# A decoder block's column stage: three engines' order written by hand, two threshold searches advanced by a budget

## The chip, the cores and the metric

One Trainium2 chip, one of its cores. A core has TensorE (matrix products; PE in the profile, PEld its weight loads), VectorE (DVE), ScalarE (ACT), GpSimd (POOL) and SyncE (SP), which issues most transfers. The metric is the device time of one execution in microseconds (us). Before: 1518.09 us, the median of 3 runs (1517.33 to 1519.06).

## The reference, cut to what matters

A decoder block over 1024 tokens of 1024 features: a sparse attention branch (an indexer scores all earlier tokens, and each query attends only to its 256 best) and a gated short convolution are merged by sigmoid gates; then 32 experts of a two-level router.

```
proj = h @ w_in
q, k, v, qi, ki, wi, conv_in, conv_b, conv_c, gates = split(proj)
rel = relu(einsum('bqhd,bsd->bqhs', qib, ki) * 64 ** -0.5)
score = einsum('bqhs,bqh->bqs', rel, wib) * 8 ** -0.5        # where admissible
_, idx = lax.top_k(score, 256)                               # attention over idx only
conv = conv_b * short_conv(conv_c * conv_in, conv_w)         # width 3, per channel
g_attn, g_conv = split(sigmoid(gates + gate_bias))
merged = g_attn * (attn @ w_attn_up) + g_conv * (conv @ w_conv_up)
h = layer_norm(alpha * h + merged @ w_out)
h = layer_norm(alpha * h + experts(h))                       # 32 experts, top 2 of a group
```

## The kernel before, in words

Matrix products run in three parts for precision: each operand is split into a high part (a rounding copy on ScalarE) and a low part (raw minus high, on VectorE or GpSimd). `mm3` (lines 141 to 144) issues high by high, high by low (of the tokens) and low by high. Eight pairs `xh`, `xl` hold the transposed input in the pool `big`, whose 16 pages (tag `er`) later hold raw expert weights.

The order of the stages: projections of keys, values and indexer; scores `sc` for query blocks 2 to 7 (per head and 512 keys two matmuls, a Relu `rl` on ScalarE, line 277, and an accumulation into `score` on VectorE, line 281); the **column stage**; attention, with eight more columns (`gattn`) as filling work for TensorE; merge, normalisation, router; experts, whose weights stream from memory.

The column stage computes 128 output columns of `w_in` at a time for all tokens. Column j is loaded by `load_col` (raw `cr`, high part `ch` on ScalarE at line 129, low part `cl` on GpSimd at line 133, both into pages of tag `w`, of which there are five) and multiplied by `proj_col`: two halves of 512 tokens, 24 matmuls each, into a PSUM bank `pc`, which `use` then reads out. The program runs over the columns 0, 1, then 3, 4, 2, then 6, 7, 5, then 9, 10, 8, then 11, and then 12 to 19. Of a convolution triple, the first (`conv_c`) is copied out by ScalarE into `cc`; the second (`conv_in`) is multiplied into `cc` by VectorE, which then forms the three-tap filter `y` (lines 435 to 437); the third (`conv_b`), one triple late, is multiplied into `y` by VectorE and split into `convh` (ScalarE) and `convl` (GpSimd). A gate column 12 to 19 is read out through a Sigmoid into `g` by ScalarE (line 460), and is followed by 24 matmuls `pu` of the convolution with an up-projection weight `uw` (copy on ScalarE, low part on GpSimd). With eight such tiles the stage has 20 x 48 + 8 x 24 = 1152 matmuls.

The indexer's 256 best of a query are found by a threshold: `topk` bisects 16 bits of the score's upper half, then 16 of the lower. It runs twice: for blocks 2, 3, 4 by counting on VectorE (`count`, line 346), for blocks 5, 6, 7 by sums of signs on ScalarE (`sign_sums`, line 320: three sums of 768, 896 and 1024 elements and six activations of one column for each bit), with preparation and a final pass (lines 395 to 401) on VectorE. Both are issued with a late priority (`prio(LATE)`) behind the column stage in the program; the framework's scheduler chooses the order of each engine in this stage from priorities and its own model, so that the searches fill what is free. From attention on, TensorE's order is the program's (`manual_schedule`).

PSUM tiles come in tags: `f` (2 banks), `l` (3), `tr` (2), `pv` (1). The scores and the columns both take `l`.

Of the kernel before, what the change touches and what calls it, by code (L numbers as in the profile page):

```python
# [11 lines left out]
I16 = mybir.dt.int16  # L12
# [33 lines left out]
ROWS_AT = (0, 4)  # L46
HOLD = 50
NSQ = 2
OHB = 8
# [23 lines left out]
def build(tc, I, out):  # L73
# [224 lines left out]
    def topk(blocks, scalar=False):  # L298
# [7 lines left out]
        if not scalar:  # L306
            acc = psf("acc", (P, ng), "pv")
        hi, lo, msk = [tmp(n, I32) for n in ("thi", "tlo", "msk")]
# [9 lines left out]
        def sign_sums(dt, b, o):  # L318
            for i in range(ng):
                nc.scalar.activation(signs[:, :L[i]], key[i].bitcast(dt), AF.Sign, bias=b[:, i:i + 1], scale=1.0,  # L320
                                     accum_out=o[:, i:i + 1])

        def descend_signs(name, base, dt, above=None):
# [8 lines left out]
            for bit in range(15, -1, -1):  # L332
                sign_sums(dt, b, total)
                for i in range(ng):
                    nc.scalar.activation(sign[:, i:i + 1], total[:, i:i + 1], AF.Sign, bias=least[:, i:i + 1],
                                         scale=1.0)
                if bit:
                    for i in range(ng):
                        nc.scalar.activation(b[:, i:i + 1], sign[:, i:i + 1], AF.Identity, bias=b[:, i:i + 1],
                                             scale=-float(1 << bit) / 2)  # L340
# [3 lines left out]
        def count(op, dt, c, o):  # L344
            for i in range(ng):
                V.tensor_scalar(junk[:, :L[i]], key[i].bitcast(dt), c[:, i:i + 1], None, op0=op, op1=OP.add,
                                accum_out=o[:, i:i + 1])

        def descend(name, base, dt, above=None):
            if scalar:  # L350
                return descend_signs(name, base, dt, above)
            c = tmp(name)
            V.memset(c, base + 32768.0)
            for bit in range(15, -1, -1):
                count(OP.is_ge, dt, c, cnt)
                if above is not None:
                    V.tensor_tensor(cnt, cnt, above, op=OP.add)
                step = float(1 << bit)
# [3 lines left out]

        for i, t in enumerate(blocks):
            h = score[t].bitcast(I16)[:, 1::2]
            m = scratch[:, :L[i]].bitcast(I16)
            V.tensor_scalar(m, h, 0.0, 32767.0, op0=OP.is_lt, op1=OP.mult)
            V.tensor_tensor(key[i].bitcast(I16), h, m, op=OP.bitwise_xor)
        th = descend("th", -32768.0, I16)
        above = tmp("above")
        if scalar:  # L370
            V.tensor_scalar(acc, th, -1.0, -0.5, op0=OP.mult, op1=OP.add)
            sign_sums(I16, acc, above)
        else:
            count(OP.is_gt, I16, th, above)
        V.tensor_scalar(neg, th, 0.0, None, op0=OP.is_lt)
        V.tensor_scalar(sg, neg, -2.0, 1.0, op0=OP.mult, op1=OP.add)
        V.tensor_scalar(off, neg, 65535.0, None, op0=OP.mult)
        for i, t in enumerate(blocks):
            low = score[t].bitcast(U16)[:, 0::2]
            V.tensor_scalar(scratch[:, :L[i]], low, sg[:, i:i + 1], off[:, i:i + 1], op0=OP.mult, op1=OP.add)  # L380
            V.scalar_tensor_tensor(key[i], key[i].bitcast(I16), th[:, i:i + 1], scratch[:, :L[i]], op0=OP.is_equal,
                                   op1=OP.mult)
        tl = descend("tl", 0.0, U16, above)
        V.tensor_copy(hi, th)
# [6 lines left out]
        for i, t in enumerate(blocks):  # L391
            s = score[t]
            T = hi.bitcast(F32)[:, i:i + 1]
            jk, cm = scratch[:, :L[i]], key[i]
            V.tensor_scalar(jk, s, T, None, op0=OP.is_gt, op1=OP.add, accum_out=cnt[:, i:i + 1])
            V.tensor_scalar(jk, s, T, None, op0=OP.is_equal)
            V.tensor_scalar(need[:, i:i + 1], cnt[:, i:i + 1], -1.0, float(TOPK), op0=OP.mult, op1=OP.add)
            V.tensor_tensor_scan(cm, jk, jk, 0.0, op0=OP.add, op1=OP.bypass)
            V.scalar_tensor_tensor(cm, cm, need[:, i:i + 1], jk, op0=OP.is_le, op1=OP.mult)
            V.scalar_tensor_tensor(s, s, T, cm, op0=OP.is_gt, op1=OP.add)  # L400
            nc.scalar.activation(s, s, AF.Copy, bias=NEG, scale=-NEG)


# [7 lines left out]
    def proj_col(j, use):  # L411
        h, l = load_col(j)
        for n in range(2):
            c = slice(n * 512, n * 512 + 512)
            p = psf("pc", tag="l")
            for k in range(KT):
                mm3(p, h[:, k], l[:, k], xh[k][:, c], xl[k][:, c], k == 0, k == KT - 1)
            use(p, c)

# [37 lines left out]
    def gconv_tile(j):  # L457
# [4 lines left out]
        for n in range(2):  # L462
            c = slice(n * 512, n * 512 + 512)
            p = psf("pu")
            for _ in up_half(uw, lambda k: convh[k][:, c], lambda k: convl[k][:, c], n, p):
                pass
            nc.vector.tensor_tensor(g[:, c], p, g[:, c], op=OP.mult)  # L467
        nc.sync.dma_start(gc_d[j], g)
# [43 lines left out]

    for c in range(5):
        if c < 4:
            conv_in(c)
        if c > 0:
            conv_out(c - 1)
    for j in range(8):
        gconv_tile(j)

# [83 lines left out]

    with prio(LATE):
        topk([5, 6, 7], True)
        topk([2, 3, 4])
    tensor_order = ExitStack()
# [773 lines left out]
```

## Time and profile before

| | |
|---|---|
| median of 3 runs | 1518.09 us |
| profiled execution, its own time | 1517.83 us |
| its span, first to last instruction | 1516.0 us |
| mean granted TensorE clock | 0.966 |
| PE busy | 1416.2 us (93%) |
| DVE busy | 1101.3 us (73%) |
| ACT busy | 997.2 us (66%) |
| POOL busy | 399.6 us (26%) |

Busy shares are means over stages with different limits, so they don't say what a change in one stage is worth; the rows further below are of the column stage and its neighbours. A bracket in a row of the timeline gives the idle time before the instruction and what ended it. A busy TensorE is not TensorE at full speed: its clock has two levels, and matmuls overlap, so that their pitch (start to start) and not their duration is what a column costs.

### The profile page before, as it was taken

The page shows a single profiled execution, that of the slowest core. Times are in us where ns is not written, and L with a number is a line of the kernel's source. Part 1 is how long each engine was busy: PE and PEld are TensorE (multiplying, and loading weights), DVE is VectorE, ACT ScalarE, POOL GpSimd, SP SyncE. Part 2 cuts the span into 40 slices and gives each one's busy share as a digit, 9 for nine tenths or more (in the row PEclk, how much of TensorE's full clock was granted, in tenths as well). Part 3 has the DMA queues.
Part 4 walks back from the last instruction along what each step waited for, and adds up shares of the span by engine and source line. Part 5 has one row for each costly group of instructions (what it writes and reads, how often), then busy time and mean ns, then how long its engine had stood idle before and what let it go on. Part 6 is the DMA issues. An engine that isn't in the chain of part 4 may idle for free. (4 is left out here: it accounts for less than half of the span.)

```text
span 1516.0 us, 20432 instructions
## 1 busy us (share of the span) xinstructions
PE 1416.2 (93%) x6746; PEld 1158.7 (76%) x6746; DVE 1101.3 (73%) x1913; ACT 997.2 (66%) x1657; POOL 399.6 (26%) x346
## 2 busy tenths in 40 slices
PE   7999899899998999988999499999999999999993
PEld 7887687678877888866788477777777777777773
DVE  5354999960616666657634889889998889888876
ACT  5444788589326666555432378888888888888864
POOL 2433112232324555324000511111111111111106
PEclk9999899999999999989999699999999999999997
DMA  5201211112112121335854678999999999999942
GB/s 192 70 21 58 88 44 42 42 42 84 56 65 75 50 84 57 105 119 180 303 205 171 238 260 273 362 365 369 365 372 364 367 360 362 360 357 363 365 196 112
DMA packets 97053, 301.78 MB, mean 199 GB/s; under 512 B 14670, under 2 KB 19150, under 8 KB 96944
## 3 DMA queue, kind: packets, MB, share of 16 engines
q1 hardware_dynamic: 88160, 284.28, 51.1%
q0 software_dynamic: 8784, 16.16, 4.3%
q8 instruction: 54, 0.88, 0.2%
q14 instruction: 55, 0.45, 0.1%
HBM read 276.12 MB, written 40.11 MB: 209 GB/s over the span
## 5 line engine op out<-in xcount | busy, mean ns | idle before, releaser
L133 DVE TENSOR_TENSOR el<-er,eh 128x1024 fp32r<-128x1024 f32 x376 | 447.6, 1222 | 52.6 <-ACT eh L129 47.5
L129 ACT ACTIVATE eh<-er 128x1024 fp32r<-128x1024 f32 x376 | 390.7, 1062 | 62.8 <-PE gu L144 31.1
L142 PE MATMUL gu<-eh,exh 128*128 128x512 f32 x512 | 208.4, 407 | 0.0
L144 PE MATMUL gu<-eh,exl 128*128 128x512 f32 x512 | 202.9, 396 | 0.0
L143 PE MATMUL gu<-el,exh 128*128 128x512 f32 x512 | 202.7, 396 | 0.0
L142 PE MATMUL pc<-xh,ch 128*128 128x512 f32 x448 | 180.7, 403 | 11.0 <-DVE cc L433 8.9
L144 PE MATMUL pc<-xh,cl 128*128 128x512 f32 x448 | 175.8, 395 | 1.3 <-POOL cl L133 1.3
L143 PE MATMUL pc<-xl,ch 128*128 128x512 f32 x448 | 176.8, 395 | 0.0
L1044 POOL DMA_INDIRECT y_d<-yo,gidx x29 | 46.1, 1588 | 436.8 <-ACT yo L1036 422.5
L144 PEld LDWEIGHTS gu<-eh,exl 128*128 128x128 f32 x512 | 96.4, 188 | 23.4 <-DVE exl L133 0.2
L143 PEld LDWEIGHTS gu<-el,exh 128*128 128x128 f32 x512 | 96.8, 189 | 20.4
L142 PEld LDWEIGHTS gu<-eh,exh 128*128 128x128 f32 x512 | 96.7, 189 | 20.6 <-ACT exh L129 0.4
L142 PEld LDWEIGHTS pc<-xh,ch 128*128 128x128 f32 x448 | 85.3, 190 | 26.9 <-DVE cc L433 9.8
L133 POOL TENSOR_TENSOR cl<-cr,ch 128x1024 fp32r<-128x1024 f32 x28 | 67.4, 2408 | 138.5 <-PE pc L144 119.0
L142 PE MATMUL py<-eh,hT 128*128 128x512 f32 x256 | 101.3, 396 | 0.0
L143 PE MATMUL py<-el,hT 128*128 128x512 f32 x256 | 101.2, 395 | 0.0
L144 PE MATMUL py<-eh,hT 128*128 128x512 f32 x256 | 101.2, 395 | 0.0
L144 PEld LDWEIGHTS pc<-xh,cl 128*128 128x128 f32 x448 | 85.3, 190 | 20.5 <-POOL cl L133 1.8
L559 POOL TENSOR_TENSOR p<-p,mx 128x128 f32<-128x128 f32 (+7 forms) x64 | 73.0, 1148 | 92.7 <-DVE mx L558 56.2
L143 PEld LDWEIGHTS pc<-xl,ch 128*128 128x128 f32 x448 | 85.4, 191 | 13.7
L281 DVE SCALAR_TENSOR_TENSOR score<-rl,wis,score 128x512 f32<-128x512 f32 (+1 forms) x70 | 51.0, 750 | 34.6 <-ACT rl L277 33.4
L467 DVE TENSOR_TENSOR g<-pu,g 128x512 f32<-128x512 f32 x16 | 11.0, 689 | 84.5 <-ACT g L460 43.5
(336 smaller groups left out, 3105.1 us busy)
## 6 DMA issues: line engine op xcount, KB each, us to landing
er<-in_w_e SPq DMA_DIRECT2D x384, 512.0 KB
cr<-in_w_ct SPq DMA_DIRECT2D x28, 512.0 KB
gc_d<-g SPq DMA_DIRECT2D x8, 512.0 KB
ga_d<-g SPq DMA_DIRECT2D x8, 512.0 KB
ur<-in_w_au SPq DMA_DIRECT2D x16, 256.0 KB
gg<-ga_d SPq DMA_DIRECT2D x16, 256.0 KB
gg<-gc_d SPq DMA_DIRECT2D x16, 256.0 KB
wor<-in_w_out SPq DMA_DIRECT2D x8, 512.0 KB
```

The costliest lines, as they stand in the source:

```text
L129: exps["last"] = nc.scalar.activation(hi, src, AF.Copy).ins
L133: i = eng.tensor_tensor(lo, src, hi.bitcast(F32), op=OP.subtract)
L142: nc.tensor.matmul(ps, sh, mh, start=start, stop=False)
L143: nc.tensor.matmul(ps, sh, ml, start=False, stop=False)
L144: return nc.tensor.matmul(ps, sl, mh, start=False, stop=stop).ins
L281: nc.vector.scalar_tensor_tensor(sc[:, n0:n1], rl, wis[:, t, h:h + 1], sc[:, n0:n1], op0=OP.mult, op1=OP.add)
L467: nc.vector.tensor_tensor(g[:, c], p, g[:, c], op=OP.mult)
L559: nc.gpsimd.tensor_tensor(p[:, :L], p[:, :L], mx[:, 0:1].to_broadcast([P, L]), op=OP.mult)
L1044: nc.gpsimd.indirect_dma_start(out=y_d, out_offset=bass.IndirectOffsetOnAxis(ap=si, axis=0), in_=yo, in_offset=None, bounds_check=S - 1, o ...
```

## The change

Three parts. The column stage goes into a block in which TensorE, VectorE and ScalarE all run in the program's order (GpSimd and the transfers stay with the scheduler). The two searches become generators: they yield, before each step, the engine and an estimated cost, and `search(2.8)`, called in the middle and at the end of each half projection of the columns from 2 on and after each half of `pu`, advances both until 2.8 us x 0.6 of ScalarE or 2.8 us x 0.8 of VectorE are spent; what is left runs after the last tile. And the columns 0, 1, 3 and 4 take PSUM tag `f`, and the raw pages of columns 0 and 1 take tag `w`, so that neither waits for what the scores use. A small part: the `above` counts of the VectorE search are kept in PSUM (`over`).

```diff
+SHARE = {"act": 0.6, "dve": 0.8}
+EARLY_COLS = (0, 1, 3, 4)
...
         def sign_sums(dt, b, o):
             for i in range(ng):
+                yield "act", 0.45 + L[i] / 1000
                 nc.scalar.activation(signs[:, :L[i]], key[i].bitcast(dt), AF.Sign, bias=b[:, i:i + 1], scale=1.0,
                                      accum_out=o[:, i:i + 1])
...
             for bit in range(15, -1, -1):
-                sign_sums(dt, b, total)
+                yield from sign_sums(dt, b, total)
...
         def count(op, dt, c, o):
             for i in range(ng):
+                yield "dve", 0.4 + L[i] / 1000
                 V.tensor_scalar(junk[:, :L[i]], key[i].bitcast(dt), c[:, i:i + 1], None, op0=op, op1=OP.add,
                                 accum_out=o[:, i:i + 1])
...
+    searches = {}
+
+    def search(us):
+
+        left = {n: us * SHARE[n] + searches.get(n, 0.0) for n in SHARE}
+        for name in ("scalar", "vector"):
+            while name in searches:
+                gen, step = searches[name]
+                if step is not None:
+                    if left[step[0]] <= 0:
+                        break
+                    left[step[0]] -= step[1]
+                step = next(gen, None)
+                searches[name] = gen, step
+                if step is None:
+                    searches.pop(name)
+        for n in SHARE:
+            searches[n] = min(0.0, left[n])
...
     def proj_col(j, use):
-        h, l = load_col(j)
+        h, l = load_col(j, "w" if j < 2 else "a")
         for n in range(2):
             c = slice(n * 512, n * 512 + 512)
-            p = psf("pc", tag="l")
+            p = psf("pc", tag="f" if j in EARLY_COLS else "l")
             for k in range(KT):
                 mm3(p, h[:, k], l[:, k], xh[k][:, c], xl[k][:, c], k == 0, k == KT - 1)
+                if k == KT // 2 - 1 and j > 1:
+                    search(2.8)
+            if j > 1:
+                search(2.8)
             use(p, c)
...
             for _ in up_half(uw, lambda k: convh[k][:, c], lambda k: convl[k][:, c], n, p):
                 pass
+            search(2.8)
             nc.vector.tensor_tensor(g[:, c], p, g[:, c], op=OP.mult)
...
-    for c in range(5):
-        if c < 4:
-            conv_in(c)
-        if c > 0:
-            conv_out(c - 1)
-    for j in range(8):
-        gconv_tile(j)
+    searches["vector"] = topk([2, 3, 4]), None
+    searches["scalar"] = topk([5, 6, 7], True), None
+    with tc.manual_schedule(engines={ET.PE, ET.DVE, ET.Activation}):
+        for c in range(5):
+            if c < 4:
+                conv_in(c)
+            if c > 0:
+                conv_out(c - 1)
+        for j in range(8):
+            gconv_tile(j)
+        search(1.0e6)
...
-    with prio(LATE):
-        topk([5, 6, 7], True)
-        topk([2, 3, 4])
```

On ScalarE, where columns 0 and 1 of the kernel before are under way (the two `cc` are column 0's halves), the order of before has the second read-out of column 0 and behind it a `ch`, which is that of column 4, the fourth in the program's order; the `ch` of columns 0, 1 and 3 stand further up.

```order
L320 ACTIVATE signs,ths_3208<-keys,thb_3207 128x768
L339 ACTIVATE thb_3207<-thg_3209,thb_3207 128x1
L320 ACTIVATE signs,ths_3208<-key,thb_3207 128x896
L335 ACTIVATE thg_3209<-ths_3208,thl_3210 128x1
L432 ACTIVATE cc<-pc 128x512
L129 ACTIVATE ch<-cr 128x1024
L320 ACTIVATE signs,ths_3208<-key,thb_3207 128x1024
```

After the change, on ScalarE at the end of column 6 (its two `cc`) and the start of column 7, the next in the program's order:

```order
L324 ACTIVATE signs,ths_1889<-key,thb_1888 128x1024
L339 ACTIVATE thg_1890<-ths_1889,thl_1891 128x1 x3
L343 ACTIVATE thb_1888<-thg_1890,thb_1888 128x1 x3
L324 ACTIVATE signs,ths_1889<-keys,thb_1888 128x768
L469 ACTIVATE cc<-pc 128x512
L131 ACTIVATE ch<-cr 128x1024
L324 ACTIVATE signs,ths_1889<-key,thb_1888 128x896
```

The `ch` behind the second `cc` is now that of the column that TensorE takes next. At every other boundary it is the same: the `ch` of a column stands behind all that the column before it put on ScalarE, for columns 3i + 2 behind `convh convh`, for a gate column behind the second `g`, the sums of two `search` calls and the `uw` copy.

On VectorE after the change, behind the end of column 4 (the two last of the filter's three operations) up to where column 2's first half is read out (`y<-pc`):

```order
L473 SCALAR_TENSOR_TENSOR y<-cc,cw,y 128x1023
L474 SCALAR_TENSOR_TENSOR y<-cc,cw,y 128x1022
L351 TENSOR_SCALAR junk,cnt_1863<-keys,th_1938 128x640
L366 TENSOR_SCALAR acc<-cnt_1863 128x3
L367 SCALAR_TENSOR_TENSOR th_1938<-acc,th_1938 128x3
L351 TENSOR_SCALAR junk,cnt_1863<-keys,th_1938 128x384
L351 TENSOR_SCALAR junk,cnt_1863<-keys,th_1938 128x512
L351 TENSOR_SCALAR junk,cnt_1863<-keys,th_1938 128x640
L366 TENSOR_SCALAR acc<-cnt_1863 128x3
L367 SCALAR_TENSOR_TENSOR th_1938<-acc,th_1938 128x3
L351 TENSOR_SCALAR junk,cnt_1863<-keys,th_1938 128x384
L483 TENSOR_TENSOR y<-pc,y 128x512
```

Ahead of the filter stands the last `cc<-pc` of column 4; behind this `y<-pc` follow two counts with two small operations, a whole bit (three counts, two small operations) and the `y<-pc` of column 2's second half. In the order of before, the counts had no fixed place beside the columns.

On TensorE before, column 0 begins behind the last of 64 score matmuls of blocks 6 and 7:

```order
L274 MATMUL sc<-kiT,qiT 128x512
L275 MATMUL sc<-kiT,qiT 128x512
L142 MATMUL pc<-xh,ch 128x512
L143 MATMUL pc<-xl,ch 128x512
L144 MATMUL pc<-xh,cl 128x512
```

After the change, column 0 begins ahead of those 64, right behind the projections `pj`:

```order
L146 MATMUL pj<-wh,xl 128x512
L144 MATMUL pc<-xh,ch 128x512
L145 MATMUL pc<-xl,ch 128x512
L146 MATMUL pc<-xh,cl 128x512
L144 MATMUL pc<-xh,ch 128x512
L145 MATMUL pc<-xl,ch 128x512
L146 MATMUL pc<-xh,cl 128x512
L276 MATMUL sc<-kiT,qiT 128x512
L277 MATMUL sc<-kiT,qiT 128x512
L144 MATMUL pc<-xh,ch 128x512
L276 MATMUL sc<-kiT,qiT 128x384
L277 MATMUL sc<-kiT,qiT 128x384
```

The 144 matmuls of columns 0, 1 and 3 are now spread among the 64; the last eight score matmuls stand behind the last matmul of column 3, and column 4 behind them.

## Rows read from the trace of the kernel before

**Rows 1.** Busy time by stage: scores, first columns, the rest of the column stage.

```profile
144.70:173.30 28.60, 22.84 (x65) 13.85 (x63) 26.36 (x36) 19.56 (x34) 7.37 (x6) 0.76 0.31 101
173.30:206.10 32.80, 32.80 (x145) 27.14 (x145) 31.31 (x79) 28.52 (x73) 4.82 (x2) 1.00 0.20 65
206.10:335.00 128.90, 116.61 (x494) 94.30 (x493) 117.44 (x296) 93.32 (x236) 36.12 (x20) 0.96 0.13 42
335.00:452.20 117.20, 117.20 (x520) 96.89 (x519) 31.93 (x42) 63.43 (x146) 27.51 (x16) 1.00 0.19 68
```

The columns are the stretch and its length, then busy us and instructions of PE, PEld, DVE, ACT and POOL, the granted clock, the share of the transfer engines and GB/s.

**Rows 2.** Timeline of PE: start, us, instruction; the first column.

```profile
173.33 0.50 PE L142 MATMUL pc<-xh,ch 128*128 128x512 f32 x1
173.67 0.39 PE L143 MATMUL pc<-xl,ch 128*128 128x512 f32 x1
...
179.81 0.39 PE L143 MATMUL pc<-xl,ch 128*128 128x512 f32 x1
```

**Rows 3.** Timeline of ACT: two copies `ch`, one bit of the sign search.

```profile
148.00 1.06 ACT L129 ACTIVATE ch<-cr 128x1024 fp32r<-128x1024 f32 x1 [0.77 <-DMA cr<-in_w_ct]
...
185.00 0.59 ACT L432 ACTIVATE cc<-pc 128x512 f32<-128x512 f32 x1
185.48 1.06 ACT L129 ACTIVATE ch<-cr 128x1024 fp32r<-128x1024 f32 x1
...
188.29 0.93 ACT L320 ACTIVATE signs<-keys,thb 128x768 int16<-128x768 int16 x1
...
190.61 1.15 ACT L320 ACTIVATE signs<-key,thb 128x1024 int16<-128x1024 int16 x1
...
192.48 0.93 ACT L320 ACTIVATE signs<-keys,thb 128x768 int16<-128x768 int16 x1
```

**Rows 4.** Timeline of POOL: low parts of columns and of the convolution.

```profile
149.14 2.36 POOL L133 TENSOR_TENSOR cl<-cr,ch 128x1024 fp32r<-128x1024 f32 x1 [0.75 <-ACT ch L129]
...
195.40 2.42 POOL L133 TENSOR_TENSOR cl<-cr,ch 128x1024 fp32r<-128x1024 f32 x1 [8.47 <-PE pc L144]
...
231.18 1.29 POOL L133 TENSOR_TENSOR convl<-y,convh 128x512 fp32r<-128x512 f32 x1 [11.61 <-ACT convh L129]
232.44 2.40 POOL L133 TENSOR_TENSOR cl<-cr,ch 128x1024 fp32r<-128x1024 f32 x1
```

**Rows 5.** Groups by line and shape, 140 to 470 us: busy us, mean ns.

```profile
L129 ACT ACTIVATE convh<-y 128x512 fp32r<-128x512 f32 x8 | 5.0, 627 | 18.7 <-DVE y L446 18.7
...
L446 DVE TENSOR_TENSOR y<-pc,y 128x512 f32<-128x512 f32 x8 | 5.5, 681 | 0.0
...
L437 DVE SCALAR_TENSOR_TENSOR y<-cc,cw,y 128x1022 f32<-128x1022 f32 x4 | 5.1, 1281 | 0.0
...
L367 DVE TENSOR_TENSOR key<-score,signs 128x896 int16<-128x896 int16 x1 | 1.1, 1084 | 0.0
```

**Rows 6.** Timeline of DVE: score accumulations, then one bit of the counts.

```profile
149.47 3.68 DVE L281 SCALAR_TENSOR_TENSOR score<-rl,wis,score 128x384 f32<-128x384 f32 x3 [0.53 <-ACT rl L277]
...
156.26 0.75 DVE L281 SCALAR_TENSOR_TENSOR score<-rl,wis,score 128x512 f32<-128x512 f32 x1 [0.20 <-ACT rl L277]
...
181.33 0.61 DVE L346 TENSOR_SCALAR_CACHE_REDUCE junk<-keys,th 128x384 uint16<-128x384 int16 x1
...
184.09 0.61 DVE L346 TENSOR_SCALAR_CACHE_REDUCE junk<-keys,th 128x384 uint16<-128x384 int16 x1
```

**Rows 7.** Timeline of PE behind its longest wait in the column stage.

```profile
299.55 0.79 PE L142 MATMUL pc<-xh,ch 128*128 128x512 f32 x1 [6.09 <-DVE cc L433]
...
303.12 0.39 PE L144 MATMUL pc<-xh,cl 128*128 128x512 f32 x1
```

**Rows 8.** Timeline of ACT: a wait, and the copy behind it.

```profile
389.98 0.85 ACT L401 ACTIVATE score<-score 128x768 f32<-128x768 f32 x1 [5.80 <-DVE score L400]
390.73 1.04 ACT L129 ACTIVATE ch<-cr 128x1024 fp32r<-128x1024 f32 x1
```

**Rows 9.** Instructions on the expert weights' raw pages: issues, ns, first and last start.

```profile
L1077 SPq DMA_DIRECT2D er<-in_w_e x380: 327/328/1165, 735.0 to 1443.0; - x190
```

More of the change, by code (lines that the diff above doesn't have):

```diff
@@ L306, in topk @@
         if not scalar:
-            acc = psf("acc", (P, ng), "pv")
+            pa = psf("acc", (P, 2 * ng), "pv")
+            acc, over = pa[:, :ng], pa[:, ng:]
         hi, lo, msk = [tmp(n, I32) for n in ("thi", "tlo", "msk")]
@@ L350, in descend @@
             if scalar:
-                return descend_signs(name, base, dt, above)
+                return (yield from descend_signs(name, base, dt, above))
             c = tmp(name)
+            if above is not None:
+                V.tensor_copy(over, above)
             V.memset(c, base + 32768.0)
             for bit in range(15, -1, -1):
-                count(OP.is_ge, dt, c, cnt)
+                yield from count(OP.is_ge, dt, c, cnt)
                 if above is not None:
-                    V.tensor_tensor(cnt, cnt, above, op=OP.add)
+                    V.tensor_tensor(cnt, cnt, over, op=OP.add)
                 step = float(1 << bit)
@@ L363, in topk @@
         for i, t in enumerate(blocks):
+            yield "dve", L[i] / 500
             h = score[t].bitcast(I16)[:, 1::2]
@@ L367, in topk @@
             V.tensor_tensor(key[i].bitcast(I16), h, m, op=OP.bitwise_xor)
-        th = descend("th", -32768.0, I16)
+        th = yield from descend("th", -32768.0, I16)
         above = tmp("above")
@@ L371, in topk @@
             V.tensor_scalar(acc, th, -1.0, -0.5, op0=OP.mult, op1=OP.add)
-            sign_sums(I16, acc, above)
+            yield from sign_sums(I16, acc, above)
         else:
-            count(OP.is_gt, I16, th, above)
+            yield from count(OP.is_gt, I16, th, above)
         V.tensor_scalar(neg, th, 0.0, None, op0=OP.is_lt)
@@ L379, in topk @@
             low = score[t].bitcast(U16)[:, 0::2]
+            yield "dve", L[i] / 400
             V.tensor_scalar(scratch[:, :L[i]], low, sg[:, i:i + 1], off[:, i:i + 1], op0=OP.mult, op1=OP.add)
@@ L382, in topk @@
                                    op1=OP.mult)
-        tl = descend("tl", 0.0, U16, above)
+        tl = yield from descend("tl", 0.0, U16, above)
+        yield "dve", 1.5
         V.tensor_copy(hi, th)
@@ L394, in topk @@
             jk, cm = scratch[:, :L[i]], key[i]
+            yield "dve", L[i] / 300
             V.tensor_scalar(jk, s, T, None, op0=OP.is_gt, op1=OP.add, accum_out=cnt[:, i:i + 1])
             V.tensor_scalar(jk, s, T, None, op0=OP.is_equal)
+            yield "dve", L[i] / 300
             V.tensor_scalar(need[:, i:i + 1], cnt[:, i:i + 1], -1.0, float(TOPK), op0=OP.mult, op1=OP.add)
             V.tensor_tensor_scan(cm, jk, jk, 0.0, op0=OP.add, op1=OP.bypass)
+            yield "dve", L[i] / 300
             V.scalar_tensor_tensor(cm, cm, need[:, i:i + 1], jk, op0=OP.is_le, op1=OP.mult)
             V.scalar_tensor_tensor(s, s, T, cm, op0=OP.is_gt, op1=OP.add)
+            yield "act", L[i] / 800
             nc.scalar.activation(s, s, AF.Copy, bias=NEG, scale=-NEG)
+    searches = {}
[14 more added lines that the diff above has]
+            searches[n] = min(0.0, left[n])
     def load_col(j, rtag="a"):
```

## The prediction

> **What bounds the kernel now.** I read the busy times by stage first. In the column stage TensorE is the bound: in its second half it is busy 117.2 us of 117.2 at full clock, in its first 32.8 us it never stops, and only between 206.1 and 335.0 does it stand idle, 12.3 us of 128.9 [rows 1]. The timeline of PE gives its pitch at full speed: 27 matmuls start between 173.67 and 179.81, which is 0.2274 us each [rows 2]. The stage's 1152 matmuls are worth 262.0 us at that pitch; from 173.33 to 452.2 they took 278.9. So 16.9 us are lost, all behind the first three columns (144 x 0.2274 = 32.7 us, which ends at 206.1).
>
> In the stretch ahead of it, the scores of blocks 6 and 7, VectorE sets the pace: busy 26.4 us of 28.6, while TensorE works 22.8 us at a mean granted clock of 0.76 [rows 1]. Here TensorE's time is nearly free: 64 score matmuls take 28.6 us that need some 13.7.
>
> What the reader should see next is how far ahead of TensorE the columns are split. Column 4 starts on TensorE at 206.1; its `ch` is made at 185.48 [rows 3], its `cl` at 195.40 [rows 4]. The split leads its column by ten to twenty us. This lead is what the new order touches.
>
> **The change, part by part.** *The scores.* The 144 matmuls of columns 0, 1 and 3 move between the score matmuls. TensorE then has 32.7 + 13.7 = 46.5 us of work from 144.7 on and is the bound, so it ends at 191.2; between columns 0 and 1 the chain read-out, `ch`, `cl` (below, 4.3 us) is covered for 2.5 us by score matmuls, so 193.0. Before, this work was done at 206.1: 13.1 us are won. But column 4 cannot start then. ScalarE's order ahead of `ch` of column 4 begins with a sign sum, which needs VectorE's keys of blocks 5 to 7 and, behind them, the memsets. VectorE ends the scores about 1.5 us after TensorE (a Relu, an accumulation of 0.75 [rows 6]); then come one filter operation of 1.28 and the keys, three operations of 1.08 [rows 5], three that I take at 0.6 and small ones of 0.7 in all, 7.0 together: 201.6. Then ScalarE: four sign sums, six small activations, two read-outs `cc` and `ch`. One bit of three sums and six small activations takes 4.19 (188.29 to 192.48), of which the small ones are 1.1; a fourth sum is 0.9, the read-outs go at 0.5 (185.00 to 185.48) and `ch` is 1.06 [rows 3]: 7.2 us, 208.8. `cl` takes 2.4 and starts 0.08 behind its `ch` (148.00 + 1.06 to 149.14) [rows 3, 4]. Its third matmul starts at 211.3, and as two need no `cl`, column 4 starts in effect at 210.8: **4.7 us later** than the 206.1 of before. Bounds: 13 us earlier if the hole were filled, some 8 later if the scores run slower.
>
> *Boundaries behind a ScalarE read-out* (columns 3i to 3i + 1; three of them behind column 4). ScalarE waits for TensorE's last matmul, reads out (0.59), makes `ch` (1.06) [rows 3], GpSimd makes `cl` (2.40) [rows 4], three hand-overs of 0.08, less the two matmuls (0.45): 3.84 us in which TensorE stands. Three are **11.5**.
>
> *Boundaries behind a convolution output* (2 to 6, 5 to 9, 8 to 11). VectorE's `y` (0.68), `convh` (0.63) [rows 5], `convl` (1.26 from start to start), `cl` (2.40) [rows 4], hand-overs 0.33, less 0.45: 4.85. On top VectorE is late. From the end of column 4 it has to do `cc` (0.6), the filter (3.1, from 1.28 an operation [rows 5]), a count of 640 with its small ones (1.3), a bit (2.76, 181.33 to 184.09 [rows 6]), a count (0.65), `y` (0.6), then 2.1 for two counts and 2.76 for a bit: 13.9 us, where column 2 takes 48 x 0.2274 = 10.9. So its last `y` starts 3.0 late; for columns 5 and 8, where the budget cuts the bits elsewhere, 2.4 and 2.1. Three boundaries: **22.1**. Behind column 11 there is also the low part of `uw` (as `convl`, 1.3), and `y` stands behind counts that follow a wait for ScalarE's thirty-second sum, 3.1 late: **9.3**. The remaining boundaries (4 to 2, 7 to 5, 10 to 8) cost nothing: the column ahead is read out by VectorE, so `ch` waits only for 7 us of sums, which fit in the 10.9.
>
> *Gate tiles.* Behind a column ScalarE reads out `g` (0.6), does one bit (4.19), `uw` (0.55), GpSimd the low part (1.3) and `cl` (2.4), with hand-overs 9.3; TensorE has 24 matmuls `pu` (5.46) and two of the next column (0.45): it stands 3.4 behind tiles 12, 14, 16. Behind 13, 15, 17 the bit lacks its sum of 896 (1.0): 2.4. Behind 18 `uw` and `ch` stand behind `score5`, which waits until VectorE has read out the first half of `pu` and done two more operations (some 5.2 behind the column) and takes 0.85 [rows 8]: 5.2 + 0.85 + 0.55 + 1.3 + 2.4, less 5.46 and 0.45, is 4.4. **21.8.**
>
> *The clock.* Behind the 6.09 us wait TensorE made 8 matmuls in 3.57 us (299.55 to 303.12) [rows 7], half its full clock (1.2 for 2.4 GHz), where 1.82 is due: 1.75 a long wait. Eight long waits (column 4's, three, four): 14.0. For the seven at the tiles, two short waits each, I find no row; between 0 and 1.75 I take 0.6: 4.2. **18.2.**
>
> *Attention's start.* About a dozen VectorE operations of the final pass land among its first units. Between nothing (TensorE has filling columns) and 8 us I take **2**, nearer to nothing as the operations stand one by one between others. The PSUM copy of `above` and the loads of two columns ahead of time cost nothing: VectorE and the queues wait for the columns.
>
> **Sum**: 4.7 + 11.5 + 22.1 + 9.3 + 21.8 + 18.2 + 2.0 = 89.6; the loss of 16.9 falls away: **+72.7**. The profiled execution took 1517.8, the median is 1518.1: I predict **1590**.
>
> **Rivals.** *Smaller.* VectorE is not late (its counts run while TensorE stands), and no wait but the bare ones counts: 4.7 + 11.5 + 14.6 + 6.2 + 21.8 - 16.9 = +41.9, **1560**. For it: waits give VectorE time to catch up. Against: the filter is at the end of a column with no wait behind it.
>
> *Larger.* `cl` and VectorE get in each other's way. Three accumulations beside a `cl` took 3.68 us, 1.23 each, where one alone takes 0.75 [rows 4, 6]; 1.7 us on each of 14 boundaries is +24, **1614**. Against: only operations like those, which read two tiles, show it; the bit from 181.33 was beside none. [...]
>
> *Faster.* ScalarE does the copy `ch` ahead of the read-out, since its inputs have long landed. Then nothing but the columns' own work is left: 13.1 won at the scores and the 16.9 lost before, **1488**. It decides below (16.9 - 4.7) / 14 = 0.87 us a boundary; one `cl` alone is 2.40. Against: at 389.98 ScalarE stood 5.80 us for `score`, and `ch` came right behind it, not during the wait [rows 8]. The Trainium skill (TensorE: Matmul & The Clock Gate, the table at its head) calls ScalarE's queue a strict FIFO. By that rule this rival is out; the trace agrees, with the 5.80.
>
> *No change.* The delay is taken up later, since the expert weights' stream bounds the second half. 380 of its loads run from 735.0 to 1443.0 [rows 9]. Against: their pages are those of `xh` and `xl`, which the filling columns read, so the stream moves with the columns. It would be **1518**.
>
> **How the numbers follow.** The forecast has 0.50, the smaller sum 0.28, the larger 0.09, the faster 0.09, no change 0.04. The range of 1552 to 1612 leaves out the last two and half of the larger. A difference of 0.2% (3 us) is about what a measurement can tell here: faster 0.09, same 0.04, slower 0.87.
>
> **What the profile after would show.** Each column's first matmul but those of 2, 5 and 8 waits for ACT `ch`, its third for POOL `cl`, about 4 us for 3i + 1, 7 to 8 for 6, 9, 11 and 12, 2 to 4 at the tiles; the granted clock between column 4 and the end falls to about 0.9. A hole of some 15 us stands between the scores and column 4. The last `pu` ends near 523. Right but mis-sized if the waits are there and shorter; wrong if `ch` runs before `cc` is read out, or if attention starts before 455.

## The result: 1605.5 us, 5.9% slower, and where the time is

The kernel after takes 1605.47 us (median of 4 runs, 1600.77 to 1609.64), the kernel before beside it 1517.71 (4 runs, 1510.45 to 1519.06): a ratio of 1.0589 with a 95% interval of 1.0565 to 1.0613. The forecast was 1590, with a range of 1552 to 1612. The profiled execution is the longest of the four, 1609.64 us with a span of 1607.8, which is 91.8 more than the span of before; the working below is made in it. The granted clock fell from 0.966 to 0.941, and PE is busy for 1445.3 us (90%), 29 us more, with the same 6746 matmuls.

Busy time by stage, the answer to [rows 1]: the scores with the first columns and the hole; columns 4 to 8 and the wait ahead of column 11; columns 11 and 12; the tiles; attention's start. In a row stand the stretch, its length, busy us and instructions of PE, PEld, DVE, ACT and POOL, granted clock, share of the transfer engines, GB/s.

```profile
142.50:211.50 69.00, 48.89 (x209) 39.41 (x207) 41.99 (x69) 28.70 (x55) 6.64 (x6) 0.87 0.16 50
211.50:343.00 131.50, 103.25 (x386) 80.07 (x386) 89.80 (x240) 73.96 (x186) 28.64 (x15) 0.86 0.10 33
343.00:378.00 35.00, 26.77 (x92) 20.84 (x93) 18.18 (x51) 15.85 (x33) 6.27 (x5) 0.79 0.12 38
378.00:534.40 156.40, 136.33 (x541) 107.63 (x540) 40.30 (x85) 89.85 (x213) 30.83 (x19) 0.91 0.16 53
534.40:570.00 35.60, 26.14 (x136) 21.00 (x135) 31.67 (x109) 19.89 (x55) 15.63 (x21) 0.86 0.16 52
```

Before, TensorE never stopped in the second half of the stage; now every stretch has holes in it, and the clock is at 0.79 to 0.91. In the column stage no other engine is full: it is waiting, not work. (At attention's start VectorE is busy for 31.67 of 35.60 us.) The largest waits of PE from 140 to 560 us (total, times, longest):

```profile
PE pc L144 <- ACT ch L131: 49.2, 12, 17.7
PE pc L146 <- POOL cl L135: 25.3, 14, 2.4
PE tr L628 <- POOL p L601: 4.3, 2, 3.5
```

Nearly all of it is a column's first matmul that waits for `ch` and its third that waits for `cl`, as forecast. The longest is the hole ahead of column 4:

```profile
211.58 0.80 PE L144 MATMUL pc<-xh,ch 128*128 128x512 f32 x1 [17.71 <-ACT ch L131]
...
214.01 0.80 PE L146 MATMUL pc<-xh,cl 128*128 128x512 f32 x1 [1.21 <-POOL cl L135]
```

The boundary from column 2 to column 6 shows how it goes; first TensorE, the answer to [rows 7]:

```profile
242.86 0.79 PE L144 MATMUL pc<-xh,ch 128*128 128x512 f32 x1 [5.56 <-ACT ch L131]
...
245.57 0.79 PE L146 MATMUL pc<-xh,cl 128*128 128x512 f32 x1 [1.49 <-POOL cl L135]
246.16 0.63 PE L144 MATMUL pc<-xh,ch 128*128 128x512 f32 x1
...
251.28 0.61 PE L144 MATMUL pc<-xh,ch 128*128 128x512 f32 x1
251.71 0.42 PE L145 MATMUL pc<-xl,ch 128*128 128x512 f32 x1
251.97 0.39 PE L146 MATMUL pc<-xh,cl 128*128 128x512 f32 x1
```

Two waits, and behind them matmuls at a pitch of 0.43 and not 0.23 us until 251.7. VectorE and then ScalarE in the same time:

```profile
235.17 0.69 DVE L483 TENSOR_TENSOR y<-pc,y 128x512 f32<-128x512 f32 x1
235.78 0.74 DVE L351 TENSOR_SCALAR_CACHE_REDUCE junk<-keys,th 128x512 uint16<-128x512 int16 x1
...
240.52 0.68 DVE L483 TENSOR_TENSOR y<-pc,y 128x512 f32<-128x512 f32 x1
...
241.76 0.75 DVE L351 TENSOR_SCALAR_CACHE_REDUCE junk<-keys,th 128x512 uint16<-128x512 int16 x1
```

```profile
241.23 0.63 ACT L131 ACTIVATE convh<-y 128x512 fp32r<-128x512 f32 x1 [2.62 <-DVE y L483]
241.77 1.04 ACT L131 ACTIVATE ch<-cr 128x1024 fp32r<-128x1024 f32 x1
```

TensorE was through with column 2 at 237.3 (242.86 less 5.56), yet the last `y` starts at 240.52: VectorE spent 235.78 to 240.5 on counts that its order puts ahead. Then `convh`, and only then `ch`, although ScalarE stood 2.62 us idle ahead of `convh` (that `ch` could run half a column earlier is shown below, by e1_lead). The rest of the chain is `convl` and `cl` on GpSimd.

A tile's boundary, ScalarE and then TensorE (column 13):

```profile
378.72 0.69 ACT L497 ACTIVATE g<-pc,gbias 128x512 f32<-128x512 f32 x1 [1.35 <-PE pc L146]
379.31 0.93 ACT L324 ACTIVATE signs<-keys,tlb 128x768 int16<-128x768 uint16 x1
...
383.79 0.61 ACT L131 ACTIVATE uw<-ur 128x512 fp32r<-128x512 f32 x1
384.31 1.04 ACT L131 ACTIVATE ch<-cr 128x1024 fp32r<-128x1024 f32 x1
```

```profile
385.40 0.50 PE L144 MATMUL pc<-xh,ch 128*128 128x512 f32 x1 [1.28 <-ACT ch L131]
...
388.12 0.69 PE L146 MATMUL pc<-xh,cl 128*128 128x512 f32 x1 [1.99 <-POOL cl L135]
```

Between the read-out `g` and the two copies stands a whole bit of the search (three sums and their small operations), 4.5 us; the 24 matmuls `pu` don't cover it.

**The sum, term by term.** A wait is counted as the distance between the starts of two matmuls less 0.2274 us; what matmuls without a wait take above 0.2274 is the clock's. All in us, the forecast's working being that above.

| term | forecast | measured |
|---|---|---|
| column 4 starts late, against 206.1 | 4.7 | 7.5 |
| boundaries behind a ScalarE read-out | 11.5 (three) | 7.4 (two of 3.7) |
| boundaries behind a convolution output | 22.1 | 22.1 (7.61, 7.25, 7.24) |
| 11 to 12 | 9.3 | 8.6 |
| tiles | 21.8 | 21.9 |
| clock | 18.2 | 31.0 |
| attention's start | 2.0 | 6.2 |
| merge and later | 0 | 4.0 |
| loss of before that falls away | -16.9 | -16.9 |
| sum | 72.7 | 91.8 |

Column 4's third matmul starts at 214.01, in effect 213.6. Attention's start is 5.6 from the end of the last `pu` to the merge's first matmul `mix` (817.0 - 534.4 = 282.6 against 729.2 - 452.2 = 277.0) and 0.6 for eight transposes of it that now lie ahead of the last `pu` (491.27 to 491.89). From there to the end it takes 4.0 more (790.8 against 786.8), most of it in the merge, where the granted clock is 0.96 and not 1.00, first after, then before:

```profile
840.00:926.00 86.00, 85.14 (x435) 71.68 (x434) 37.43 (x109) 24.44 (x43) 1.20 (x2) 0.96 0.51 183
```

```profile
752.00:835.00 83.00, 82.33 (x435) 69.43 (x435) 37.60 (x109) 24.65 (x43) 1.20 (x2) 1.00 0.53 190
```

The same 435 matmuls take 3 us longer. This is in some of the profiled executions below and not in others, and its cause stays open. The sum meets the 91.8 between the spans.

### The profile page after: what moved, and what is told of

Read it like the earlier page. It is cut to its first block, busy times and chain, and to the rows that moved or that the text cites. A ratio compares the mean times of both kernels' runs of the same rounds, so it can differ in the third digit from the quotient of the medians.

```text
span 1607.8 us, 20417 instructions
## 1 busy us (share of the span) xinstructions
PE 1445.3 (90%) x6746; PEld 1175.9 (73%) x6746; DVE 1097.9 (68%) x1914; ACT 1002.1 (62%) x1657; POOL 400.6 (25%) x346
## 5 line engine op out<-in xcount | busy, mean ns | idle before, releaser
L144 PE MATMUL pc<-xh,ch 128*128 128x512 f32 x448 | 193.4, 432 | 49.2 <-ACT ch L131 49.2
L146 PE MATMUL pc<-xh,cl 128*128 128x512 f32 x448 | 189.7, 423 | 25.3 <-POOL cl L135 25.3
L145 PE MATMUL pc<-xl,ch 128*128 128x512 f32 x448 | 187.6, 419 | 0.0
L144 PEld LDWEIGHTS pc<-xh,ch 128*128 128x128 f32 x448 | 92.6, 207 | 70.1 <-ACT ch L131 55.1
L146 PEld LDWEIGHTS pc<-xh,cl 128*128 128x128 f32 x448 | 91.9, 205 | 53.4 <-POOL cl L135 32.8
L145 PEld LDWEIGHTS pc<-xl,ch 128*128 128x128 f32 x448 | 92.2, 206 | 15.8
```

Source lines behind the costliest of these rows:

```text
L144: nc.tensor.matmul(ps, sh, mh, start=start, stop=False)
L145: nc.tensor.matmul(ps, sh, ml, start=False, stop=False)
L146: return nc.tensor.matmul(ps, sl, mh, start=False, stop=stop).ins
```

## The experiments

Theory: what costs is the place of the split in ScalarE's written order, behind the read-out of the column before and behind the search. Rivals: VectorE, late with its budget; the hand-written order as such; the other banks. Ratios are to the kernel before, run beside each on the same chip, with a 95% interval.

**The splits ahead (e1_lead).** The program writes the load and split of the next column in the middle of each first half.

```diff
-        h, l = load_col(j, "w" if j < 2 else "a")
+        if j not in ahead:
+            ahead[j] = load_col(j, "w" if j < 2 else "a")
+        h, l = ahead.pop(j)
...
+                if n == 0 and k == KT // 2 - 1 and j in FOLLOWS:
+                    f = FOLLOWS[j]
+                    ahead[f] = load_col(f, "w" if f < 2 else "a")
```

> Each column's load and split (ch, cl) is written out in the middle of the first half of the column ahead of it; everything else as in the kernel after. Theory (the split stands behind the read-out in ScalarE's fixed order, so TensorE waits at each boundary): the 61.6 us of waits behind column 4's start, the some 30 us of half clock behind them and the hole of 17.7 ahead of column 4 all go; about 1495, at most 1515, and no wait for ch or cl over 1 us from column 4 on. Rival 1 (VectorE, late with the searches' budget, holds up the boundaries): only the hole, the boundaries behind a ScalarE read-out (7.4) and the tiles (21.8) with half of the clock go; waits of 3 us and more stay at columns 6, 9, 11 and 12; about 1545. Rival 2 (the hand-written order as such costs the time): over 1580.

Measured: 1522.5 us (7 runs, 1517.6 to 1526.5), ratio 1.0049 (1.0030 to 1.0069). With this one edit the kernel is 9 us above the kernel before run beside it (1513.6), where the kernel after is 88 above. From column 4's start to column 19, waits for `ch` and `cl` are 3.1 us in all, where they were 56. VectorE's budget is untouched, so VectorE can't hold up the boundaries by itself; that the order as such costs most of the time is out. But it is some 27 us off the 1495 of the theory, and the waits show half of that, from 170 to 450 us:

```profile
PE pc L146 <- ACT cc L478: 13.1, 1, 13.1
PE pu L146 <- ACT uw L133: 3.2, 1, 3.2
PE pc L148 <- POOL cl L137: 2.3, 2, 2.0
```

The hole ahead of column 4 has moved to another resource: column 4's split is there, but the bank that it wants is read out late, since ScalarE's order has sign sums ahead of column 3's `cc`, and these wait for VectorE's keys:

```profile
199.92 0.94 ACT L326 ACTIVATE signs<-keys,thb 128x768 int16<-128x768 int16 x1 [8.38 <-DVE thl L335]
...
202.02 0.58 ACT L478 ACTIVATE cc<-pc 128x512 f32<-128x512 f32 x1
```

Another part lies behind the columns: the last `pu` ends at 447.1, 5.1 earlier than before, and from there to the first `mix` it takes 283.6 us (730.7), 6.6 more than before.

**ScalarE left to the scheduler (e2_act_free).**

```diff
-    with tc.manual_schedule(engines={ET.PE, ET.DVE, ET.Activation}):
+    with tc.manual_schedule(engines={ET.PE, ET.DVE}):
```

> The hand-written order holds for TensorE and VectorE only; ScalarE's order is made by the scheduler again. Theory (ScalarE's order is what costs): the scheduler puts ch far ahead of its column as it did in the kernel before; the waits for ch and cl shrink to under 10 us in all; 1500 to 1530. Rival 1 (VectorE's order and lateness): the waits at columns 6, 9, 11 and 12 stay, 1570 or more. Rival 2 (the order on TensorE as such): 1590 or more.

Measured: 1514.48 us (10 runs, 1510.7 to 1518.2), ratio 0.9996 (0.9982 to 1.0009). Waits for `ch` and `cl` are gone. With TensorE's and VectorE's order still written by hand, the time is that of before: the order of ScalarE made 87 of the 88 us (1 is left, each against the kernel before run beside it). That the other two orders are free doesn't follow, since this kernel has the other banks as well, which by themselves win 12 (e4_banks_only, below). A part of what they cost shows here, a bank that waits for its `y`, from 140 to 560 us:

```profile
PE pc L144 <- DVE y L483: 8.2, 2, 4.6
```

**No search in columns 0, 1 and 3 (e3_search_later).**

```diff
-                if k == KT // 2 - 1 and j > 1:
+                if k == KT // 2 - 1 and j not in (0, 1, 3):
                     search(2.8)
-            if j > 1:
+            if j not in (0, 1, 3):
                 search(2.8)
```

> No budget is given out in columns 0, 1 and 3, so that no sign sum stands ahead of ch of column 4 in ScalarE's order; nothing else is changed. Theory (the hole ahead of column 4 comes of the sums, which wait for the keys): the wait of 17.7 falls to 1 to 5, column 4 starts near 196 and not at 211.6, and the time falls by 12 to 16 us, to some 1591; the other waits stay as they are. Rival (the hole comes of the scores, which VectorE ends too late for the read-outs): the wait stays over 12 us and the time changes by under 4 us.

Of the three, only column 3 had a budget. Measured: 1588.69 us (4 runs, 1587.3 to 1589.5), ratio 1.0485 (1.0466 to 1.0505), 75 us above the kernel before. Column 4 starts at 195.24 and not at 211.58:

```profile
195.24 0.50 PE L144 MATMUL pc<-xh,ch 128*128 128x512 f32 x1 [2.12 <-ACT ch L131]
```

The hole came of the search's steps in column 3: sums ahead of `ch` on ScalarE, which wait for VectorE's keys.

**The banks alone (e4_banks_only).** The kernel before, with the early columns' banks and pages and nothing else of the change.

```diff
-        h, l = load_col(j)
+        h, l = load_col(j, "w" if j < 2 else "a")
...
-            p = psf("pc", tag="l")
+            p = psf("pc", tag="f" if j in (0, 1, 3, 4) else "l")
```

> The kernel before with one part of the change: columns 0, 1, 3 and 4 in the other PSUM banks, the raw weights of columns 0 and 1 in other pages; order by the scheduler, as before. Theory (the banks are free of cost, the order is what costs): between 1500 and 1519, faster by as much of the 13 us at the scores as the scheduler takes. Rival (the other banks cost by themselves, the scores and the columns waiting for each other's banks): over 1525.

Measured: 1501.27 us (4 runs, 1501.0 to 1504.8), ratio 0.9917 (0.9896 to 0.9938). This part of the change is a gain of 12 to 13 us by itself, near the 13.1 that the forecast gave to the scores; the last `pu` ends at 439.7, 12.5 earlier than before. So the 88 us of the whole change are net of it: against this kernel the loss is about 100, of which ScalarE's order makes 87 and the rest of the change, the two other orders and the searches' budgets, 13 (1514.48 against 1501.27). Of the 16.9 between the two profiled spans, 9.9 lie between the last `pu` and the first `mix`.

**Both edits (e5_lead_later)**: e1_lead and e3_search_later together.

> The two edits together: each column's split written half a column and more ahead, and no budget in columns 0, 1 and 3. Theory (the wait of 13.1 that the first of them still showed ahead of column 4 is the read-outs of column 3 behind the sign sums in ScalarE's order, which holds the PSUM bank): that wait goes, 1509 (1504 to 1514), and it is faster than the kernel before. Rival (the hole only moves: the sums that start later end later, and attention waits for them): 1518 or more.

Measured: 1510.53 us (10 runs, 1507.0 to 1513.6), ratio 0.9971 (0.9954 to 0.9989). The wait of 13.1 is gone (0.7 is left for `cc`), and the last `pu` ends at 431.2, 21.0 earlier than before. The span is only 5.4 shorter, though: from the last `pu` to the first `mix` it takes 289.3 us (720.5), 12.3 more than before. Most of what is won in the columns is lost in attention.

**The last passes earlier (e6_lead_later_final, e8_final_only)**, on top of e5_lead_later, and alone on the kernel after.

```diff
-            yield "act", L[i] / 800
+            yield ("act" if scalar else "dve"), L[i] / 800
...
-                search(2.8)
+                search(1.0e6 if j == 19 else 2.8)
```

> As the run with both edits, and the last passes of the search come out earlier: the vector search's read-modify step of ScalarE is charged to VectorE's budget, and what is left is written out in column 19. Theory (the 10 us that are lost between the last pu and attention come of VectorE's last passes, which run then): 5 to 10 us less than the run with both edits, about 1501. Rival (attention's first units are slow of themselves): within 2 us of it.

> The kernel after, with only the last passes of the search written out earlier (the vector search's step of ScalarE charged to VectorE's budget, the rest written out in column 19). Theory (some 10 us are lost at attention's start to VectorE's last passes): 5 to 10 us less, about 1598; the waits in the columns stay. Rival (attention's start is slow of itself): 1603 to 1608.

Measured: e6 1508.42 us (10 runs, 1505.9 to 1513.1), ratio 0.9955 (0.9939 to 0.9971); e8 1598.76 (4 runs, 1597.9 to 1601.5), ratio 1.0550 (1.0514 to 1.0586). For e8, whose interval overlaps that of the kernel after, the profiles decide, one of each: from the last `pu` (536.1) to the first `mix` (809.5) it takes 273.4 us, 9.2 fewer than after, so the loss at attention's start is back and some more. In the kernel after VectorE stood idle in tile 19 with this work undone, and did it when attention began:

```profile
531.91 0.69 DVE L505 TENSOR_TENSOR g<-pu,g 128x512 f32<-128x512 f32 x1 [11.93 <-PE pu L146]
```

The code says why: the budget gives the search on ScalarE its turn first, and the other, at a step charged to ScalarE, found nothing left. VectorE's part of block 2 was done at 395.8, the step of ScalarE behind it ran at 505.50, and blocks 3 and 4 came only then. In tile 19 the code prices a step of 896 elements at 2.99 us, more than the 2.24 that a call gives VectorE. (e8 makes two edits, the charge and the writing out in column 19; they were not tried one by one.) In e6 the expectation failed. There the columns are so short that ScalarE's last sum ends at 420.3, 13 us ahead of the last `pu`, and the last passes are not done in time. ScalarE's order has the read-outs `g` of column 19 (446.39) behind a `score` step that waits 6.69 us for VectorE's last pass, VectorE's `g` stands behind these, and TensorE waits for the bank (140 to 500 us); from the last `pu` to the first `mix` it takes 288.0, hardly fewer than in e5_lead_later:

```profile
PE pc L146 <- DVE g L514: 13.8, 1, 13.8
```

So where the last lines stand isn't enough; that the search itself is too long for the shorter columns is tried by e9 below.

**The clock kept up (e7_keep_clock).** The kernel after, with idle matmuls of live operands into a bank that nobody reads.

```diff
+    def idle(n):
+        if n:
+            spare = psf("idle", tag="tr")
+            for i in range(n):
+                nc.tensor.matmul(spare, xh[0][:, :P], xh[0][:, :512], start=i == 0, stop=i == n - 1)
...
+        idle(IDLE.get(j, 0))
...
+                    idle(6)
```

> The kernel after, with matmuls of the same operands into a spare bank, whose result nobody reads, put where TensorE waits: 4 to 21 ahead of a column's first matmul, 6 ahead of its third, from column 6 on; the output is unchanged. Theory (behind each wait TensorE runs at half its clock for some matmuls, 30 us in all, because it stood): the waits for ch and cl are filled, the clock stays at full, and the time falls by 20 to 28 us, to about 1580, with ch and cl made at the same distance behind their column as before. Rival (the slow matmuls are slow for another reason, or the fillers push the columns back): within 6 us of 1605, or slower.

Measured: 1582.50 us (4 runs, 1581.9 to 1583.0), ratio 1.0443 (1.0407 to 1.0479). TensorE at column 6:

```profile
242.81 0.39 PE L450 MATMUL idle<-xh 128*128 128x512 f32 x1
244.02 0.50 PE L460 MATMUL pc<-xh,ch 128*128 128x512 f32 x1 [0.81 <-ACT ch L133]
244.35 0.40 PE L461 MATMUL pc<-xl,ch 128*128 128x512 f32 x1
244.59 1.53 PE L450 MATMUL idle<-xh 128*128 128x512 f32 x6
246.76 0.50 PE L463 MATMUL pc<-xh,cl 128*128 128x512 f32 x1 [0.64 <-POOL cl L137]
247.10 0.40 PE L146 MATMUL pc<-xh,ch 128*128 128x512 f32 x1
```

The column starts as late as ever, but its matmuls follow each other at 0.23 us at once. From column 4's third matmul to the last `pu` it takes 296.6 us, 23.8 fewer than after (534.4 - 214.01 = 320.4). That is what keeping the clock up gives back. Slow matmuls still cost 5.0 us (1.6 behind column 4, which has no fillers) where they cost 31.0, 26.0 less; fillers and waits together take 61.7 us where the waits took 60.0.

**VectorE's lateness (e10_no_counts).** The kernel after, with no budget for VectorE in columns 2, 5 and 8 and a double one in the tiles.

```diff
-    def search(us):
+    def search(us, dve=1.0):
...
-        left = {n: us * SHARE[n] + searches.get(n, 0.0) for n in SHARE}
+        left = {n: us * SHARE[n] * (dve if n == "dve" else 1.0) + searches.get(n, 0.0) for n in SHARE}
...
+COUNTS = {2: 0.0, 5: 0.0, 8: 0.0, **{j: 2.0 for j in range(12, 20)}}
```

> The kernel after, with no budget for VectorE in columns 2, 5 and 8; in the tiles, where VectorE mostly stands idle, it is doubled instead. Theory (of the 22.1 us that TensorE waits at columns 6, 9 and 11, 14.6 are the bare chain y, convh, convl, cl, and 7.5 VectorE's counts ahead of y): 13.5 to 15.5 us of waits at the three columns together, the others unchanged; some 1597, if attention's start stays as it was. Rival (VectorE is not late; ScalarE's sums or GpSimd make up the 22.1): they stay at 21 to 23, and the time within 3 us of 1605.

Measured: 1589.23 us (4 runs, 1586.8 to 1592.0), ratio 1.0513 (1.0485 to 1.0541). The second half of `y` in column 2, and TensorE at column 6:

```profile
238.47 0.69 DVE L484 TENSOR_TENSOR y<-pc,y 128x512 f32<-128x512 f32 x1 [4.75 <-PE pc L147]
```

```profile
240.82 0.50 PE L145 MATMUL pc<-xh,ch 128*128 128x512 f32 x1 [2.39 <-ACT ch L132]
...
243.54 0.80 PE L147 MATMUL pc<-xh,cl 128*128 128x512 f32 x1 [1.98 <-POOL cl L136]
```

Now VectorE waits for TensorE, and the three boundaries cost 4.70, 4.69 and 4.70, 14.1 in all, where the forecast had 4.85 for the bare chain. 8.0 us of the 22.1 were VectorE's counts. The time fell by more than that. Behind the shorter waits the clock takes 3.7 less, and the doubled budget also ends the search earlier: from the last `pu` (522.9) to the first `mix` it takes 276.3 us (799.2), 6.3 fewer than after.

**A shorter search (e9_share, e9_blocks)**, both on top of e5_lead_later with the vector search's ScalarE step charged to VectorE:

```diff
-SHARE = {"act": 0.6, "dve": 0.8}
+SHARE = {"act": 0.72, "dve": 0.8}
```

```diff
-    searches["vector"] = topk([2, 3, 4]), None
-    searches["scalar"] = topk([5, 6, 7], True), None
+    searches["vector"] = topk([2, 3, 4, 5]), None
+    searches["scalar"] = topk([6, 7], True), None
```

> The splits ahead and the searches later, as before; ScalarE's share of the budget is 0.72 and not 0.6, and the vector search's step of ScalarE is charged to VectorE's budget, so that the last sign sum is written out in tile 17 and the last pass in tile 19; nothing is left for attention's start. Theory (the run with both edits loses 15.4 us between the last pu and attention against the kernel before, because the search ends too late: 1079.2 us from the last pu to the end there, 1063.8 before): the last pu ends near 432, attention starts right behind it, 1495 to 1501. Rival (ScalarE, given 7.8 to 8.1 us of sums in a column of 10.9 beside its read-outs and ch, becomes late itself, and TensorE waits for it in the columns): 1505 or more, with waits for ScalarE at banks or splits.

> The splits ahead and the searches later; block 5 is moved from ScalarE's search to VectorE's (two blocks on ScalarE, four on VectorE), shares as in the change, the vector search's step of ScalarE charged to VectorE. Theory (the search's end is what attention's start waits for): ScalarE's sums are done in tile 16, VectorE's passes end with tile 19 but for the last of block 5; 1497 to 1503. Rival (VectorE, with a quarter more counts, is late at the convolution outputs): 1506 or more, with waits for y, convh or cc in the columns.

Measured: e9_share 1500.73 us (6 runs, 1498.2 to 1501.6), ratio 0.9902 (0.9885 to 0.9919); e9_blocks 1497.48 (6 runs, 1495.4 to 1504.5), ratio 0.9891 (0.9869 to 0.9914). Both beat both kernels, by 14 to 17 us against before; their intervals overlap with each other and with that of e4_banks_only, so which of the three is best stays open. In e9_blocks the last `pu` ends at 430.3, 21.9 earlier than before, and from there to the first `mix` (708.1) it takes 277.8 us, against 277.0 before: this time what the columns win is kept. Its largest waits of PE in the columns, 170 to 430 us:

```profile
PE pc L148 <- POOL cl L137: 4.0, 2, 2.0
PE pc L146 <- DVE y L492: 1.3, 1, 1.3
```

## Why the prediction held, and where its sizes were off

*The mechanism* was right. A strict order makes ScalarE put `ch` behind the read-out and the sums. e1_lead moves the split (and its load), e2_act_free lets the scheduler choose ScalarE's order, e3_search_later takes the search out of one column; they leave 9, 1 and 75 of the 88 us.

*Boundaries behind a convolution output* and *tiles*: 22.1 and 21.9 for 22.1 and 21.8, and e10_no_counts splits the first into 14.1 bare and 8.0 of lateness (forecast 14.6 and 7.5). That both agree to 0.1 us is luck: ahead of column 18 the wait is 1.7 for 2.4, ahead of 19 it is 5.1 for 4.4, and in the first an error of 0.5 each way cancels. With this the rival "smaller" falls, which held that VectorE is not late.

*Boundaries behind a ScalarE read-out*: the price was right (3.84, measured 3.70), the count wrong. Of the pairs 3i and 3i + 1 only 6 to 7 and 9 to 10 lie behind column 4; 4.1 us too much.

*The scores*: column 4 came 2.8 later than worked out. The step that failed is VectorE's end behind TensorE's. TensorE was done at 193.9 (193.0 forecast), but the accumulations were not 1.5 behind it: in VectorE's new order two filter operations stand among them.

```profile
194.44 1.41 DVE L283 SCALAR_TENSOR_TENSOR score<-rl,wis,score 128x512 f32<-128x512 f32 x2
195.77 1.28 DVE L473 SCALAR_TENSOR_TENSOR y<-cc,cw,y 128x1023 f32<-128x1023 f32 x1
196.96 0.75 DVE L283 SCALAR_TENSOR_TENSOR score<-rl,wis,score 128x512 f32<-128x512 f32 x1
```

The last accumulation ends at 197.7 and not at 194.5. ScalarE's part behind it, 7.2, was 7.3 (204.26 to 211.53).

*The clock* was the largest miss: 31.0 for 18.2. The one row of before, 1.75 behind a wait of 6.09, was taken for every long wait; at columns 6, 9, 11 and 12 it is 2.4 to 3.4, and the seven long waits that there are cost 17.8 where eight were put at 14.0. And "between 0 and 1.75 I take 0.6" for two short waits was the step that failed most: at the tiles it is 13.3 in all, 1.9 each, for 4.2. The trace of before had a row nearer to them, at column 5:

```profile
258.06 0.50 PE L142 MATMUL pc<-xh,ch 128*128 128x512 f32 x1 [2.84 <-DVE cc L433]
```

Behind this wait the matmuls go at 0.43 from 258.96 to 261.95, and 1.7 us are lost, as many as behind 6.09. e7_keep_clock takes 26.0 of the 31.0 away.

*Attention's start*: 6.2 for 2, and 4.0 later on for which there was no term. The reason for taking the lower end, that the operations stand one by one between others, failed. One of them, the scan of 1024 (a running sum), takes 3.90 and stands ahead of attention's first row maxima:

```profile
535.31 3.90 DVE L410 TENSOR_TENSOR_SCAN key<-signs 128x1024 uint16<-128x1024 uint16 x1
539.13 0.26 DVE L591 CUSTOM_DVE_ANT_0 p<-lg,bias 128x128 f32<-128x128 f32 x1
```

In e8_final_only this scan is done at 526.1, ahead of the last `pu`, and more than the 6.2 is back.

*The rivals.* "Larger", a collision of `cl` with the counts, is not seen: the count of 512 takes 0.74 alone and 0.75 beside `convl` (241.94 to 243.21 on GpSimd), and 23 counts of this kernel that ran beside GpSimd took, by their length, 0.61, 0.75 and 0.88 like the others. Its 1.23 was a mean of unlike parts: of the three accumulations the first took 2.44 and ended 0.4 behind the `cl`, the others 0.74 and 0.62. "Faster" fell with `ch` behind the read-outs. "No change" fell too: from the merge on nothing of the delay is taken up. The forecast was 15.5 below the median; the terms that were short add up to 12.8 + 4.2 + 4.0 + 2.8 + 0.1, those too long to 4.8, which is 19.1 in the profiled execution, itself 4.2 above the median.

## What to carry to other kernels

Before an engine's order is written by hand, list what the scheduler had run ahead, here the split of the next weights, and write it a stage earlier; in a strict order an instruction that has been ready for long stands behind one that waits for another engine. A budget for filling work must be sized by when the work has to be done, and each search must be charged to an engine on which it gets a turn; otherwise an engine stands idle beside its own backlog. And a wait of TensorE is to be priced with the half clock behind it: here 60 us of waits brought 31 more.

## What the runs showed of the hardware

Short waits cost clock as well. At column 14 TensorE did its 24 matmuls `pu` and two of the column at full clock, stood 1.99 us for `cl`, and then made eight matmuls at a pitch of 0.43, half its clock: a loss of 1.70. At column 18 it stood 1.55 and kept its clock. At column 10, behind two waits of 1.63 and 1.75, the clock held for four more matmuls and only then fell. What decides it can't be read from these rows alone.

A scan on VectorE is held up by GpSimd. The same pass over 896 elements, in the kernel after and in e1_lead:

```profile
513.56 4.04 DVE L410 TENSOR_TENSOR_SCAN key<-signs 128x896 uint16<-128x896 uint16 x1
```

```profile
434.24 2.02 DVE L412 TENSOR_TENSOR_SCAN key<-signs 128x896 uint16<-128x896 uint16 x1
```

In the first a `cl` runs beside it (GpSimd, 2.73 from 513.00, where others take 2.40), in the second GpSimd is idle. The scan of 1024 at attention's start took 3.90 beside a `cl` and 2.29 in e8_final_only without one. The two are longer by 2.02 and 1.61, about as long as they ran beside `cl` (2.17 and 1.75). The Trainium skill (SBUF — State Buffer, Who interferes with whom) says that a VectorE instruction with two SBUF inputs contends with a GpSimd one that reads SBUF; the scan has two, and the rows agree.

An operation with a single input was slowed as well, though in the prediction's rows only operations that read two tiles showed it. A comparison of 896 elements took 1.32 us beside the low part of `uw` (GpSimd, 511.77 to 513.04), one of 1024 without it 0.75:

```profile
512.21 1.32 DVE L407 TENSOR_SCALAR signs<-score,thi 128x896 uint16<-128x896 f32 x1
...
533.83 0.75 DVE L407 TENSOR_SCALAR signs<-score,thi 128x1024 uint16<-128x1024 f32 x1
```

In e1_lead the filter's first operation, with one input too, took 2.92 beside a `cl` and 0.75 at the three other columns. The Trainium skill (SBUF — State Buffer, Who interferes with whom) says that an instruction with one input can contend in modes in which it takes both ports, but not in the form that also writes out a sum. By that rule the comparison can collide and the counts can't; the rows agree.
